# A hybrid decoder layer on one core: the PSUM banks of the recursive products in a ring of five, the others in a ring of three

## The chip, the cores and the metric

The kernel runs on one core of one Trainium2 chip. The metric is the device time of one execution in microseconds (us), given as the median of several runs; smaller is better. One execution was recorded by the hardware profiler, and all times of single instructions come from it. TensorE is called PE below, VectorE DVE, ScalarE ACT, GpSimd POOL and SyncE SP.

## The reference

One layer of a decoder trunk with three parallel branches, in float32, for 1024 prompt rows and 8 sample rows (1032 in all, model width 1024):

```
z = x @ w_in                      # (1032 x 1024) @ (1024 x 7680)
xr, yr, q, k, v, xq, g = split(z)
a_out = rg_lru(conv4(xr)) * gelu(yr)
s_out = window_attention(q, k, v)         # 16 heads, 4 kv heads, window 128, sinks
c_out = memory_attention(xq, mem_kv)      # 4 heads of 256, 256 memory rows
merged = sum(sigmoid(g_n + b_n) * (branch_n @ w_branch[n]))
h = LN(alpha * x + merged @ w_out)
y = LN(alpha * h + (silu(h @ w_gate) * (h @ w_up)) @ w_down)     # hidden width 2816
```

The memory keys and values of the prompt, the updated window buffers and the states are outputs as well.

## The kernel before

Each float32 operand is split into a high and a low part, and a product is three matmuls: high by high, high by low, low by high. ACT makes the high part, DVE the low part by a subtraction (`split`, line 77 for the low part). Most products are plain ones, in `mm3` (lines 117 to 119); the projections of the input, most of gate and up, and most of down are recursive ones, in the manner of Strassen and Winograd, with seven block products in place of eight. The program calls one such piece of work a unit: 256 columns of the weight by all 1032 rows.

A unit is seven steps, i = 0 to 6, in `fast_step`. In each step and for each p of 0 and 1, `fast_product` issues 4 x 3 = 12 matmuls of 258 columns (lines 237 to 239) into one PSUM bank; p is one half of the columns. There are three sums for each p. The first, b, collects steps 0, 2, 4 and 6; d collects steps 1 and 5; c is step 3 alone. Between the steps the running sum is copied out: ACT copies b, d and b after steps 0, 1 and 2 (line 263, tiles p1s, p5s and u2s), DVE adds c to p1s after step 3 (line 265, za) and subtracts for zb after step 4 (line 267), DVE adds d to u2s after step 5 (line 270, the last reading of d), and ACT copies b after step 6 (`finish.late`, zb: lines 1608, 1629 and 1648 for gate, down and the projections). So a unit ends with d read by DVE and b read by ACT.

PSUM has eight banks. The program makes one pool of them for the whole kernel, and the method `bank` (line 71) takes a tile from one of four rings, by tag: `BANKS = {"mm": 3, "s": 2, "t": 2, "o": 1}` (line 34). A ring hands its banks out in turn. The sums b are on ring "mm" with three banks, d on "t" with two, c on "s" with two. The single bank "o" serves the smaller tiles that come between: the gate products of the recurrence, the score transposes of the decode rows (dct, line 921, and drt_c, line 872), vt and others. With three banks and two b's a unit, the second b of a unit has the bank of the first b of the unit before it.

The stages, by the recorded execution: the memory's keys and values (0 to 58 us), the projections with the recurrence and the decode rows between them (to 690 us, 30 units, in the order of the list `UNITS`), the first branch products and the memory attention (to 806), the window attention (to 1016), the last branch product, out projection and the plain part of gate and up (to 1245), the recursive part of gate, up and down (`gate_up_down`, to 1824, 28 units), and the last plain part of down with the layer norm (`last_products`, to 1908). A layer that schedules the program decides the order on each engine from the dependences and its own costs; PE's order of the window stage is set by hand. Loads of weights are issued on SP, in half rows of 512 columns.

In `last_products` the sums are called dl, and their first matmul is at line 117; its weights are made on DVE and ACT by lines 1386 and 1387, and its operands g5l, g6l and g7l by line 77. In the memory attention co is the product of the probabilities (cph and cpl) with the values.

Of the kernel before, what the change touches and what calls it, by code (L numbers as in the profile page):

```python
# [10 lines left out]
F32 = mybir.dt.float32  # L11
# [4 lines left out]
PSUM = bass.MemoryType.PSUM  # L16
DRAM = bass.MemoryType.DRAM

P = 128
# [7 lines left out]
NM = 256  # L27
# [11 lines left out]
QN = T // 4  # L39
# [19 lines left out]
class Builder:  # L59
# [9 lines left out]
        return self.slots[which].tile([P, CW[c]], F32R, tag=tag, name=name, bufs=8)[:, :CH[c][1]]  # L69

    def bank(self, tag, name):
        return self.psum.tile([P, 512], F32, tag=tag, name=name, bufs=BANKS[tag])

    def split(self, hi, lo, src):

# [68 lines left out]
    def setup(self):  # L144
        nc, ctx, tc, io = self.nc, self.ctx, self.tc, self.io
        self.cst = ctx.enter_context(tc.tile_pool(name="cst", bufs=1))
        self.psum = ctx.enter_context(tc.tile_pool(name="psum", bufs=1, space=PSUM))
        self.dram = ctx.enter_context(tc.tile_pool(name="scr", bufs=1, space=DRAM))

        self.ident = self.cst.tile([P, P], F32, name="ident")  # L150
        self.ones = self.cst.tile([P, P], F32R, name="ones")
        self.vec = self.cst.tile([P, V_N], F32, name="vec")
        nc.vector.memset(self.ones.bitcast(F32), 1.0 / D)
# [75 lines left out]
    def fast_product(self, st, i, p, ts, ps, opens):  # L229
# [5 lines left out]
        for k in range(4):  # L235
# [2 lines left out]
            mm(sh[:, w], xl, start=False, stop=False)  # L238
            self.last_mm = mm(sl[:, w], xh, start=False, stop=k == 3).ins  # L239

    def fast_step(self, st, i, ts, finish):

        nc, u, scale = self.nc, st["u"], getattr(finish, "scale", 1.0)
        cols = lambda th, p: slice(HT * th + QN * p, HT * th + QN * (p + 1))
        small = lambda tag, p: self.w1.tile([P, QN], F32, tag=tag, name=f"{tag}{u}_{p}", bufs=2)
        if i == 3:
            st["za"] = self.zt(f"za{u}")
        if i == 4:
            st["zb"] = self.zt(f"zb{u}")
        for p in range(2):  # L250
            if i == 0:
                st["b", p] = self.bank("mm", f"ub{u}_{p}")[:, :QN]
            elif i == 1:
                st["d", p] = self.bank("t", f"ud{u}_{p}")[:, :QN]
            elif i == 3:
                st["c", p] = self.bank("s", f"uc{u}_{p}")[:, :QN]
            b, c, d = st.get(("b", p)), st.get(("c", p)), st.get(("d", p))
            ps = {0: b, 1: d, 2: b, 3: c, 4: b, 5: d, 6: b}[i]
            self.fast_product(st, i, p, ts, ps, i in (0, 1, 3))
            add = partial(nc.vector.scalar_tensor_tensor, scalar=scale, op0=ALU.mult, op1=ALU.add)  # L260
            if i in (0, 1, 2):
                st["s", i, p] = small(("p1s", "p5s", "u2s")[i], p)
                self.last_copy = nc.scalar.mul(st["s", i, p], ps, scale).ins  # L263
            elif i == 3:
                add(st["za"][:, cols(0, p)], c, in1=st["s", 0, p])
            elif i == 4:
                self.last_evac = nc.vector.scalar_tensor_tensor(st["zb"][:, cols(1, p)], b, -scale, st["s", 1, p],
                                                                op0=ALU.mult, op1=ALU.subtract).ins
            elif i == 5:
                add(st["za"][:, cols(1, p)], d, in1=st["s", 2, p])  # L270
            else:
                finish.late(st["zb"][:, cols(0, p)], b)
        if i == 6:
            finish.done(st["za"], st["zb"])

# [114 lines left out]
    def mem_kv(self, moving, xs, load, quarters):  # L390


        nc, io = self.nc, self.io
        h = D // 2
        memx, raws, pairs, sums = [], {}, {}, {}
        order = [(f, p) for f in ((0, 0), (0, 1), (1, 1), (1, 0)) for p in range(2)]

        def put(ps, name, m):
            raw = self.ph.tile([P, 256], F32, tag="kvraw", name=f"{name}r{m}", bufs=4)
            nc.scalar.copy(raw, ps)  # L400
            nc.gpsimd.dma_start(self.scr[name][:, m, :], raw)

        def mem_raw(k):
            raws["mem", k] = self.half_raw(io["memT"][:, 2 * k * NM:(2 * k + 2) * NM], 2 * NM, f"mem{k}")

        def mem_split(k):
            raw = raws.pop(("mem", k))
            for i in range(2):
                memx.append(tuple(self.ph.tile([P, NM], F32R, tag="mem", name=f"mem{e}{2 * k + i}", bufs=16)
                                  for e in "hl"))  # L410
                self.split(*memx[-1], raw[:, i * NM:(i + 1) * NM])

        def fetch(n):
            if n < 16:
                src = io["wmk"][n // 2][:, n % 2 * h:(n % 2 + 1) * h]
            else:
                src = io["wmv"][(n - 16) // 2][:, n % 2 * h:(n % 2 + 1) * h]
            raws[n] = self.half_raw(src, h, f"wm{n}r")

        def cut(n):  # L420
            pairs[n] = self.half_pair(f"wm{n}_")
            self.split(*pairs[n], raws.pop(n))

        def key(n):
            m, e = n // 2, n % 2
            if e == 0:
                sums[m] = self.bank("mm", f"mk{m}")[:, :NM]
            hi, lo = pairs.pop(n)
            cols = [slice(i * P, (i + 1) * P) for i in range(4)]
            self.mm3(sums[m], [((hi[:, w], lo[:, w]), memx[4 * e + i]) for i, w in enumerate(cols)], e == 1, e == 0)  # L430

        def value(n):
            g, j = (n - 16) // 4, n % 4
            if j == 0:
                sums[g] = [self.bank("mm", f"mv{g}_{tt}")[:, :256] for tt in range(2)]
            hi, lo = pairs.pop(n)
            cols = [slice(i * 256, (i + 1) * 256) for i in range(2)]
            for tt in range(2):
                xs_ = [tuple(a[:, tt * P:(tt + 1) * P] for a in memx[2 * j + i]) for i in range(2)]
                self.mm3(sums[g][tt], [(x, (hi[:, w], lo[:, w])) for x, w in zip(xs_, cols)], j == 3, j == 0)  # L440

        warm = self.bank("o", "warm")
        for _ in range(WARM):
            nc.tensor.matmul(warm[:, :P], self.ones, self.ones, start=True, stop=True)
        for f in (partial(mem_raw, 0), partial(fetch, 0), partial(mem_raw, 1), partial(mem_raw, 2), partial(fetch, 1),
                  partial(mem_raw, 3), partial(fetch, 2), partial(fetch, 3)):
            f()
        for f in (partial(mem_split, 0), partial(cut, 0), partial(mem_split, 1), partial(mem_split, 2), partial(cut, 1),
                  partial(mem_split, 3)):
            f()  # L450
        due = -3.5
        for n in range(32):
# [12 lines left out]
            if due > 0:  # L465
                due -= next(moving)
            (key if n < 16 else value)(n)
            if 0 < n <= 16 and n % 2 == 0:
                put(sums.pop(n // 2 - 1), "mk", n // 2 - 1)
            if n > 16 and n % 4 == 0:  # L470
                g = (n - 16) // 4 - 1
                for tt, ps in enumerate(sums.pop(g)):
                    put(ps, "mv", 2 * g + tt)
        for tt, ps in enumerate(sums.pop(3)):
            put(ps, "mv", 6 + tt)
# [1055 lines left out]
    def build(self):  # L1531
        nc, tc, io = self.nc, self.tc, self.io
# [7 lines left out]
        pool = lambda name, side="left": tc.tile_pool(name=name, bufs=1, side=side, reuse_waits="tile")  # L1540
        self.wpool = self.ctx.enter_context(pool("wpool"))
        self.ctx.enter_context(pool("edge", "right")).tile([P, 8], F32, name="edge")
        self.zbufs = 9
        with pool("tp", "right") as self.tp, pool("w1") as self.w1, pool("z") as self.z, ExitStack() as late:
            self.project(late, pool)
        self.act, self.merged, self.first_gates = {}, {}, []
        with ExitStack() as right:
            slots = right.enter_context(ExitStack())
# [36 lines left out]
            with pool("zf") as self.z:  # L1585
                with ExitStack() as tx:
                    self.g, self.wl, self.wraw, self.A = [], [], [], {}
                    with pool("lnp") as self.ph:
# [2 lines left out]
                            h = self.out_proj(self.merged)  # L1591
                        self.tx = tx.enter_context(pool("tx", "right"))
                        ts = self.plain(h)
                    with pool("w1") as self.w1:
                        self.gate_up_down(ts)
                    with pool("ph5") as self.ph:
                        self.last_products()

# [178 lines left out]
```

## Time and profile before

| what | value |
|---|---|
| median of three runs | 1907.44 us (1907.36, 1907.44, 1909.93) |
| the profiled execution, whole | 1909.41 us |
| its span, first to last instruction | 1907.6 us |
| PE's mean granted clock | 0.997 |
| instructions in the span | 38153 |
| moved by DMA | 302.18 MB, 158 GB/s on the mean |

The profiled execution is 1909.41 - 1907.6 = 1.8 us longer than its span: that is time before the first and after the last recorded instruction. Rows of a timeline begin with the start and the length in us, then the engine, the line, the operation, output and inputs by their names, the shape of the output, how many instructions are merged (x2), and in brackets the idle time ahead of the row and what ended it. Rows of the list of waits name an engine and a line, what it waited for, the total in us, how often, and the longest. Rows of a group have the count, the busy time and mean ns, and behind the second bar the idle time ahead of it. Rows of windows have the stretch, its length, the busy time of PE, PE's weight loads, DVE, ACT and POOL, then PE's granted clock, the DMA share, and GB/s.

### The profile page before, as it was taken

Reading aid. Unit: us, or ns where it says so; the run is one execution under the profiler, and the core shown is the slowest. Engines: PE = TensorE matmul, PEld = TensorE weight load, DVE = VectorE, ACT = ScalarE, POOL = GpSimd, SP = SyncE. Lnnn points to the kernel's source line nnn. Section 1 sums busy time; section 2 is a strip of 40 time slices with the busy share of each in tenths; the row PEclk is TensorE's granted clock in tenths of the full one; section 3 lists DMA queues with packets and bytes.
Section 4 is the critical chain, followed back from the end, with each engine's and each line's share of the span. In section 5 each row is a group of like instructions: output and inputs, shape, how many; then the busy total and the mean of one; then the engine's idle time right before and its main releaser. Section 6 shows DMA issues by size and latency. Waiting matters only on the chain.

```text
span 1907.6 us, 38153 instructions
## 1 busy us (share of the span) xinstructions
PE 1889.4 (99%) x14878; PEld 1870.0 (98%) x14878; DVE 1389.9 (73%) x2712; ACT 1014.8 (53%) x2124; POOL 112.8 (6%) x190
## 2 busy tenths in 40 slices
PE   9999999999999999999999999999999999999998
PEld 8999999999999999999999999999999999999997
DVE  7868877977887657578887467786666667858486
ACT  6555564555665656578775234543433433636354
POOL 1000000010000000022210000000000000001200
PEclk9999999999999999999999999999999999999998
DMA  8535434546444368546435351133355335759872
GB/s 316 171 119 173 136 128 139 172 144 214 136 150 147 113 209 264 181 144 208 144 100 164 111 190 51 57 122 118 111 165 191 106 123 177 269 127 272 174 211 90
DMA packets 175973, 302.18 MB, mean 158 GB/s; under 512 B 18912, under 2 KB 92592, under 8 KB 175792
## 3 DMA queue, kind: packets, MB, share of 16 engines
q1 hardware_dynamic: 169120, 280.64, 45.0%
q0 software_dynamic: 4224, 14.78, 3.9%
q10 hardware_dynamic: 2448, 4.33, 0.6%
q8 instruction: 116, 1.90, 0.4%
q14 instruction: 65, 0.53, 0.1%
HBM read 217.97 MB, written 85.89 MB: 159 GB/s over the span
## 4 chain that ended last, share of the span: by engine, by line
PE 90%; DMA 4%; DVE 3%; ACT 2%; issue 1%; SPq 0%; DVEq 0%; ACTq 0%
PE ub L237 5%; PE ub L239 5%; PE ub L238 5%; PE ubfg L238 4%; PE ubfg L237 4%; PE ubfg L239 4%; PE ud L239 3%; PE ud L237 3%; PE ud L238 3%; PE udfg L237 2%; PE udfg L238 2%; PE udfg L239 2%; PE ubf L237 2%; PE op L117 2%; PE ubf L238 2%; PE ubf L239 2%
## 5 line engine op out<-in xcount | busy, mean ns | idle before, releaser
L645 ACT ACTIVATE bp<-bp,bst 128x257 f32<-128x257 f32 (+1 forms) x128 | 62.8, 493 | 38.5 <-DVE bst L639 37.8
L237 PE MATMUL ub<-th,u_0h 128*128 128x258 f32 x240 | 68.6, 286 | 1.0 <-ACT zb L1648 1.0
L237 PE MATMUL ub<-th,u_6h 128*128 128x258 f32 x240 | 68.7, 286 | 0.0
L237 PE MATMUL ub<-th,u_4h 128*128 128x258 f32 x240 | 68.0, 283 | 0.7 <-ACT u2s L263 0.7
L237 PE MATMUL ub<-th,u_2h 128*128 128x258 f32 x240 | 68.0, 283 | 0.4 <-ACT p1s L263 0.4
L239 PE MATMUL ub<-th,u_0l 128*128 128x258 f32 x240 | 68.0, 283 | 0.0
L639 DVE CUSTOM_DVE_ANT_0 bp<-bs,mask,nsnk 128x256 f32<-128x256 f32 (+1 forms) x128 | 55.8, 461 | 16.8 <-PE bs L636 16.4
L239 PE MATMUL ud<-th,u_5l 128*128 128x258 f32 x240 | 68.0, 283 | 0.0
L237 PE MATMUL ud<-th,u_5h 128*128 128x258 f32 x240 | 67.9, 283 | 0.0
L239 PE MATMUL ud<-th,u_1l 128*128 128x258 f32 x240 | 67.9, 283 | 0.0
L239 PE MATMUL ub<-th,u_2l 128*128 128x258 f32 x240 | 67.9, 283 | 0.0
L239 PE MATMUL uc<-th,u_3l 128*128 128x258 f32 x240 | 67.9, 283 | 0.0
L239 PE MATMUL ub<-th,u_6l 128*128 128x258 f32 x240 | 67.9, 283 | 0.0
L239 PE MATMUL ub<-th,u_4l 128*128 128x258 f32 x240 | 67.9, 283 | 0.0
L237 PE MATMUL uc<-th,u_3h 128*128 128x258 f32 x240 | 67.9, 283 | 0.0
L237 PE MATMUL ud<-th,u_1h 128*128 128x258 f32 x240 | 67.9, 283 | 0.0
L238 PE MATMUL ub<-tl,u_0h 128*128 128x258 f32 x240 | 67.6, 282 | 0.0
L238 PE MATMUL ub<-tl,u_6h 128*128 128x258 f32 x240 | 67.5, 281 | 0.0
L238 PE MATMUL ub<-tl,u_2h 128*128 128x258 f32 x240 | 67.4, 281 | 0.0
L238 PE MATMUL uc<-tl,u_3h 128*128 128x258 f32 x240 | 67.4, 281 | 0.0
L238 PE MATMUL ud<-tl,u_5h 128*128 128x258 f32 x240 | 67.4, 281 | 0.0
L238 PE MATMUL ud<-tl,u_1h 128*128 128x258 f32 x240 | 67.4, 281 | 0.0
(949 smaller groups left out, 8294.8 us busy)
## 6 DMA issues: line engine op xcount, KB each, us to landing
ur<-win SPq DMA_DIRECT2D x120, 256.0 KB, 3.2
urfg<-wgu SPq DMA_DIRECT2D x80, 256.0 KB, 2.8
scr_f<-G SPq DMA_DIRECT2D x22, 516.0 KB, 3.1
f<-scr_f SPq DMA_DIRECT2D x16, 516.0 KB, 4.9
fs<-scr_t SPq DMA_DIRECT2D x16, 516.0 KB, 5.5
dck<-cmk SPq DMA_DIRECT2D x32, 256.0 KB, 4.1
dcv<-cmvT SPq DMA_DIRECT2D x32, 256.0 KB, 4.2
urf<-wdn SPq DMA_DIRECT2D x32, 256.0 KB, 2.9
```

Source lines behind the costliest of these rows:

```text
L117: nc.tensor.matmul(ps, sh, mh, start=opens and i == 0, stop=False)
L237: mm(sh[:, w], xh, start=opens and k == 0, stop=False)
L238: mm(sh[:, w], xl, start=False, stop=False)
L239: self.last_mm = mm(sl[:, w], xh, start=False, stop=k == 3).ins
L639: nc.vector.tensor_tensor_reduce(pg[g], s[:, u * 256:u * 256 + n], msk, 1.0, snk[:, g:g + 1], ALU.add, ALU.min, st[:, g:g + 1])
L645: nc.scalar.activation(x, x, AF.Exp, bias=st[:, g:g + 1], scale=-1.0, accum_out=st[:, 4 + g:5 + g])
```

## The change

In the two stages with units, eight banks are divided otherwise. Five banks, x0 to x4, hold b and d of the units and, ahead of the first unit, the sums of the memory's keys and values. They lie in a queue `self.idle`: `take` removes the one at its front, which was handed back longest ago, and a unit hands its d banks back with step 5 and its b banks with step 6, at the back. All other tiles, c of the units, the recurrence, the transposes, are on one ring of three banks, "s".

Since the tags of the tiles differ between the stages, the one pool becomes four: psum0 for the projections, psum1 for the attentions and branch products, psum2 for gate, up and down, psum3 for the last stage. A pool's banks are opened again in the next one, and a tile waits there for the last reader of the old tile in the same bank. In psum1 and psum3 the four old tags with their counts are used.

```diff
     def bank(self, tag, name):
+        if self.idle is not None:
+            return self.psum.tile([P, 512], F32, tag="s", name=name, bufs=3)
         return self.psum.tile([P, 512], F32, tag=tag, name=name, bufs=BANKS[tag])
+
+    def take(self, name):
+        k = self.idle.popleft()
+        return k, self.psum.tile([P, 512], F32, tag=f"x{k}", name=name, bufs=1)
...
-        self.psum = ctx.enter_context(tc.tile_pool(name="psum", bufs=1, space=PSUM))
...
+    def sum_bank(self, st, tag, name):
+
+        if self.idle is None:
+            return self.bank(tag, name)[:, :QN]
+        k, ps = self.take(name)
+        st.setdefault("banks", []).append(k)
+        return ps[:, :QN]
...
             if i == 0:
-                st["b", p] = self.bank("mm", f"ub{u}_{p}")[:, :QN]
+                st["b", p] = self.sum_bank(st, "mm", f"ub{u}_{p}")
             elif i == 1:
-                st["d", p] = self.bank("t", f"ud{u}_{p}")[:, :QN]
+                st["d", p] = self.sum_bank(st, "t", f"ud{u}_{p}")
...
+        if self.idle is not None and i > 4:
+            self.idle += st["banks"][2:] if i == 5 else st["banks"][:2]
...
-            nc.scalar.copy(raw, ps)
+            nc.scalar.copy(raw, bank[1][:, :256])
+            self.idle.append(bank[0])
...
+        banks = lambda name: tc.tile_pool(name=name, bufs=1, space=PSUM, reuse_waits="tile")
         with pool("tp", "right") as self.tp, pool("w1") as self.w1, pool("z") as self.z, ExitStack() as late:
-            self.project(late, pool)
+            with banks("psum0") as self.psum:
+                self.idle = deque(range(5))
+                self.project(late, pool)
+        self.idle, psum = None, ExitStack()
+        self.psum = psum.enter_context(banks("psum1"))
...
-                    with pool("w1") as self.w1:
+                    psum.close()
+                    with pool("w1") as self.w1, banks("psum2") as self.psum:
+                        self.idle = deque(range(5))
                         self.gate_up_down(ts)
+                    self.idle, self.psum = None, self.ctx.enter_context(banks("psum3"))
```

On PE, at the border of the fourth and the fifth unit of the projections: ub4_1 is b of p=1, ud4_0 and ud4_1 are d. Before, the first matmul into each bank waits for the engine that emptied it:

```order
L239 MATMUL ub4_0_2099<-th0_0_122,u4_0l_1975 128x258
L237 MATMUL ub4_1_2114<-th0_1_124,u4_0h_1974 128x258 [waits Activation_49]
...
L239 MATMUL ub4_1_2114<-th0_1_124,u4_0l_1975 128x258
L237 MATMUL ud4_0_2145<-th1_0_126,u4_1h_2010 128x258 [waits DVE_49]
...
L237 MATMUL ud4_1_2160<-th1_1_128,u4_1h_2010 128x258 [waits DVE_49]
```

With the change, at the same place:

```order
L244 MATMUL ub4_0_2099<-th0_0_122,u4_0l_1975 128x258
L242 MATMUL ub4_1_2114<-th0_1_124,u4_0h_1974 128x258 [waits DVE_49]
...
L244 MATMUL ub4_1_2114<-th0_1_124,u4_0l_1975 128x258
L242 MATMUL ud4_0_2145<-th1_0_126,u4_1h_2010 128x258 [waits DVE_49,Activation_49]
...
L242 MATMUL ud4_1_2160<-th1_1_128,u4_1h_2010 128x258 [waits Activation_49]
```

The order of the matmuls is the same. The second b now follows DVE, which read d of the unit before, and the first d follows two engines. Over the program 49 more waits of this kind, each a semaphore instruction of its own, stand in PE's order, 46 of them at d.

On PE, at the first sum of the last stage, behind the last unit (ubf13_1). Before:

```order
L239 MATMUL ubf13_1_23574<-dth16_1_22774,uf13_6l_23694 128x258
L117 MATMUL dl0_0_23898<-g5h21_23479,wl0h00_23677 128x258 [waits Activation_49]
L118 MATMUL dl0_0_23898<-g5l21_23480,wl0h00_23677 128x258
...
L117 MATMUL dl0_0_23898<-g6h0_23589,wl0h00_23677 128x258 [waits Activation_49]
L118 MATMUL dl0_0_23898<-g6l0_23590,wl0h00_23677 128x258 [waits DVE_49]
```

With the change:

```order
L244 MATMUL ubf13_1_23582<-dth16_1_22782,uf13_6l_23702 128x258
L123 MATMUL dl0_0_23910<-g5h21_23487,wl0h00_23685 128x258 [waits DVE_49,Activation_49]
L124 MATMUL dl0_0_23910<-g5l21_23488,wl0h00_23685 128x258
...
L123 MATMUL dl0_0_23910<-g6h0_23597,wl0h00_23685 128x258 [waits Activation_49]
L124 MATMUL dl0_0_23910<-g6l0_23598,wl0h00_23685 128x258
```

The first matmul of dl0_0 now waits for DVE too; the later wait for DVE ahead of g6l0 is gone, since what the first one waits for stands behind g6l0 in DVE's order.

On DVE, at the start of the memory attention: M is the merged sum, mkl, mv and cql the low parts of keys, values and queries, wba2 the weights of a branch. Before:

```order
L721 SCALAR_TENSOR_TENSOR M1_9557<-gta1_9660,bra1_1_9766 128x390 [waits PE_49]
L77 TENSOR_TENSOR mkl0_9872<-mkl0_9872,mkh0_9871 128x512 [waits DMAHW4_49,Activation_49]
L77 TENSOR_TENSOR mv0_9874<-mv0_9874 128x512 [waits DMAHW5_49,Activation_49]
L721 SCALAR_TENSOR_TENSOR M0_9556<-gta0_9620,bra0_2_9832 128x258 [waits PE_49]
L77 TENSOR_TENSOR cql0_9877<-cql0_9877,cqh0_9876 128x1024 [waits DMAHW6_49,Activation_49]
L77 TENSOR_TENSOR wba20_l_9996<-wba2r0__9993,wba20_h_9995 128x512 [waits DMAHW0_49,DVE_49,Activation_49]
```

With the change:

```order
L83 TENSOR_TENSOR mkl0_9876<-mkl0_9876,mkh0_9875 128x512 [waits DMAHW4_49,Activation_49]
L83 TENSOR_TENSOR mv0_9878<-mv0_9878 128x512 [waits DMAHW5_49,Activation_49]
L737 SCALAR_TENSOR_TENSOR M1_9561<-gta1_9664,bra1_1_9770 128x390 [waits PE_49]
L83 TENSOR_TENSOR cql0_9881<-cql0_9881,cqh0_9880 128x1024 [waits DMAHW6_49,Activation_49]
L83 TENSOR_TENSOR mkl1_9949<-mkl1_9949,mkh1_9948 128x512 [waits DMAHW7_49,Activation_49]
L83 TENSOR_TENSOR wba20_l_10000<-wba2r0__9997,wba20_h_9999 128x512 [waits DVE_49,DMAHW0_49,PE_49,Activation_49]
```

The two additions to M move behind splits of the memory operands, and the split of the second head's keys comes ahead of that of the branch weights.

More of the change, by code (lines that the diff above doesn't have):

```diff
@@ L396, in mem_kv, with put @@
         order = [(f, p) for f in ((0, 0), (0, 1), (1, 1), (1, 0)) for p in range(2)]
-        def put(ps, name, m):
+        def put(bank, name, m):
             raw = self.ph.tile([P, 256], F32, tag="kvraw", name=f"{name}r{m}", bufs=4)
-            nc.scalar.copy(raw, ps)
+            nc.scalar.copy(raw, bank[1][:, :256])
+            self.idle.append(bank[0])
             nc.gpsimd.dma_start(self.scr[name][:, m, :], raw)
@@ L426, in key @@
             if e == 0:
-                sums[m] = self.bank("mm", f"mk{m}")[:, :NM]
+                sums[m] = self.take(f"mk{m}")
             hi, lo = pairs.pop(n)
             cols = [slice(i * P, (i + 1) * P) for i in range(4)]
-            self.mm3(sums[m], [((hi[:, w], lo[:, w]), memx[4 * e + i]) for i, w in enumerate(cols)], e == 1, e == 0)
+            self.mm3(sums[m][1][:, :NM], [((hi[:, w], lo[:, w]), memx[4 * e + i]) for i, w in enumerate(cols)], e == 1, e == 0)
         def value(n):
@@ L434, in value @@
             if j == 0:
-                sums[g] = [self.bank("mm", f"mv{g}_{tt}")[:, :256] for tt in range(2)]
+                sums[g] = [self.take(f"mv{g}_{tt}") for tt in range(2)]
             hi, lo = pairs.pop(n)
@@ L439, in value @@
                 xs_ = [tuple(a[:, tt * P:(tt + 1) * P] for a in memx[2 * j + i]) for i in range(2)]
-                self.mm3(sums[g][tt], [(x, (hi[:, w], lo[:, w])) for x, w in zip(xs_, cols)], j == 3, j == 0)
+                self.mm3(sums[g][tt][1][:, :256], [(x, (hi[:, w], lo[:, w])) for x, w in zip(xs_, cols)], j == 3, j == 0)
         warm = self.bank("o", "warm")
```

## The prediction

> **What bounds the kernel now.** First the busy shares on the page and the engines in the chain that ended last, then the windows cut at the stage borders, then what PE waits for.
>
> ```profile
> PE 1889.4 (99%) x14878; PEld 1870.0 (98%) x14878; DVE 1389.9 (73%) x2712; ACT 1014.8 (53%) x2124; POOL 112.8 (6%) x190
> ```
> ```profile
> PE 90%; DMA 4%; DVE 3%; ACT 2%; issue 1%; SPq 0%; DVEq 0%; ACTq 0%
> ```
> ```profile
> 60.00:690.00 630.00, 627.58 (x5175) 625.30 (x5174) 487.70 (x998) 361.00 (x685) 36.18 (x49) 1.00 0.46 149
> 690.00:806.00 116.00, 114.77 (x747) 107.92 (x746) 75.52 (x169) 69.93 (x172) 3.64 (x9) 1.00 0.70 232
> 1245.00:1824.00 579.00, 578.91 (x4810) 578.64 (x4809) 391.99 (x597) 254.88 (x494) 19.08 (x22) 1.00 0.55 166
> 1824.00:1908.00 84.00, 74.38 (x615) 73.74 (x614) 60.75 (x120) 39.13 (x88) 1.80 (x2) 0.94 0.40 123
> ```
> ```profile
> PE ub L237 <- ACT zb L1648: 1.0, 1, 1.0
> PE co L118 <- DVE cpl L77: 0.7, 2, 0.4
> PE dct L921 <- ACT ti L829: 0.2, 1, 0.2
> ```
>
> TensorE is the bound: 99% busy, 90% of the chain, at a granted clock of 1.00 in the stages that the change touches (the first number after POOL's in a windows row). Those are the projections (60 to 690 us, 30 units) and gate/up/down (1245 to 1824 us, 28 units). In them PE is idle for 630.00 - 627.58 = 2.4 us and 579.00 - 578.91 = 0.1 us. So freeing banks earlier can only return small holes; the longest bank wait of the whole list is the first of the three rows, 1.0 us.
>
> Busy time hides a part of each hole, because matmul rows overlap: a 258-column matmul lasts 0.28 us, yet the next starts 0.12 us later. So I read holes from start to start, less 0.12.
>
> **Part 1: b's second bank is no longer b's first bank of the unit before.** In the kernel before, the bank of p=0 of step 0 is taken again 24 matmuls after its last write, 24 x 0.12 = 2.9 us; in that time ScalarE must have copied it out. With five banks every reuse of the units stands at least 48 matmuls away, 5.8 us. Where does the old distance fall short? In the timeline of PE, the matmul ahead, the one that waits, and at the first place the one behind:
>
> ```profile
> 100.25 0.28 PE L239 MATMUL ub<-th,u_0l 128*128 128x258 f32 x1
> 101.56 0.39 PE L237 MATMUL ub<-th,u_0h 128*128 128x258 f32 x1 [1.04 <-ACT zb L1648]
> 101.79 0.29 PE L238 MATMUL ub<-tl,u_0h 128*128 128x258 f32 x1
> ...
> 228.70 0.28 PE L239 MATMUL ub<-th,u_0l 128*128 128x258 f32 x1
> 228.88 0.39 PE L237 MATMUL ub<-th,u_0h 128*128 128x258 f32 x1
> ...
> 268.31 0.28 PE L239 MATMUL ub<-th,u_6l 128*128 128x258 f32 x1
> 268.76 0.38 PE L921 MATMUL dct<-ident,dcs 128*8 128x128 f32 x2 [0.17 <-ACT ti L829]
> ...
> 274.15 0.28 PE L238 MATMUL ud<-tl,u_1h 128*128 128x258 f32 x1
> 274.32 0.39 PE L237 MATMUL ub<-th,u_0h 128*128 128x258 f32 x1
> ...
> 335.25 0.28 PE L237 MATMUL ub<-th,u_0h 128*128 128x258 f32 x1
> 335.60 0.38 PE L872 MATMUL drt_c<-ident,qdc 128*8 128x128 f32 x2
> ...
> 376.96 0.28 PE L239 MATMUL ub<-th,u_0l 128*128 128x258 f32 x1
> 377.21 0.39 PE L237 MATMUL ub<-th,u_0h 128*128 128x258 f32 x1
> ...
> 1562.21 0.29 PE L239 MATMUL ubfg<-hh,ufg_0l 128*128 128x258 f32 x1
> 1562.34 0.28 PE L237 MATMUL ubfg<-hh,ufg_0h 128*128 128x258 f32 x1
> 1562.46 0.28 PE L238 MATMUL ubfg<-hl,ufg_0h 128*128 128x258 f32 x1
> ...
> 1582.44 0.28 PE L239 MATMUL ubfg<-hh,ufg_0l 128*128 128x258 f32 x1
> 1582.82 0.39 PE L237 MATMUL ubfg<-hh,ufg_0h 128*128 128x258 f32 x1
> ```
> ```profile
> 101.15 0.36 ACT L1648 ACTIVATE zb<-ub 128x258 f32<-128x258 f32 x1
> ```
>
> At 101.56 the hole is 101.56 - 100.25 - 0.12 = 1.19 us, and the row behind comes 0.23 after it instead of 0.12, 0.11 more for refilling: 1.30 us. ScalarE's copy of that bank ends at 101.15 + 0.36 = 101.51, 0.05 ahead, so this is the bank. The other step-0 matmuls are read alike, each with the same 0.11 (an estimate from 101.79): 228.88 gives 0.06 + 0.11 = 0.17, 274.32 gives 0.05 + 0.11 = 0.16, 377.21 gives 0.13 + 0.11 = 0.24, 1582.82 gives 0.26 + 0.11 = 0.37. The transposes dct (0.45 - 0.12 = 0.33) and drt_c (0.35 - 0.12 = 0.23) wait for the single bank "o", whose place a ring of three takes. Together 1.30 + 0.17 + 0.16 + 0.24 + 0.37 + 0.33 + 0.23 = 2.8 us. Most of the boundaries between units have no hole: that at 1562.34 stands 0.13 behind the row ahead, and its next 0.12. What comes late next, once these waits are gone, is the split of the weight quarters; at none of these places is it the wait named. I take -2.8, with the ends 0 (a split is late too) and -9.5 (a rival below).
>
> **Part 2: a bank that the last stage takes too early.** The old kernel's first output sum of the last stage, dl, opened on a ring of three that was long free. Now the last pool is opened anew, its first bank is the physical bank of the last unit's d for p=0, and dl waits for DVE's read of that (the L270 row):
>
> ```profile
> 1823.82 0.28 PE L239 MATMUL ubf<-dth,uf_6l 128*128 128x258 f32 x1
> 1823.93 0.28 PE L117 MATMUL dl<-g5h,wl0h 128*128 128x258 f32 x1
> ```
> ```profile
> 1800.22 0.42 DVE L270 SCALAR_TENSOR_TENSOR zaf<-udf,u2sf 128x258 f32<-128x258 f32 x1
> ...
> 1820.98 2.37 DVE L77 TENSOR_TENSOR g7l<-g7l,g7h 128x1032 fp32r<-128x1032 f32 x2
> 1823.27 1.66 DVE L1387 SCALAR_TENSOR_TENSOR wl0l<-wl1r,wbar,wl0h 128x128 fp32r<-128x128 f32 x6
> 1824.84 0.75 DVE L270 SCALAR_TENSOR_TENSOR zaf<-udf,u2sf 128x258 f32<-128x258 f32 x2
> ```
>
> That read stands in DVE's queue behind splits of 2.37 and 1.66 us. The first of the pair starts at 1824.84 and takes 0.42 by the single row of it, to 1825.26; with the same 0.05 for release dl starts at 1825.31 instead of 1823.93, 1.38 later, and refills for 0.11: +1.5 us. Queued behind dl on PE is the whole last stage, and nothing else is there to fill the hole. If PE comes 2.8 us earlier and DVE's splits do not, since they follow DMAs, the hole grows by that, to 4.3; if DVE's queue drains before PE arrives, it is 0. The last three rows follow each other without a gap, so DVE is behind by work and not by a wait; the holes that go lie 240 us and more ahead of this place, time enough for loads and splits to move up with PE. So I take 1.5, with the ends 0 and 4.3. Each microsecond is paid once: PE is in the chain there.
>
> **Part 3: waits on two engines.** The ring mixes banks that DVE frees with banks that ScalarE frees, so 46 first matmuls of d now wait for both. Instructions with two such waits are already in the kernel: of the 60 of this row 32 wait for two engines.
>
> ```profile
> L673 PE MATMUL bo<-bph,vs 128*128 128x512 f32 x60 | 24.0, 400 | 0.2 <-ACT bph L76 0.2
> ```
>
> All 60 have 0.2 us of idle time ahead of them, 0.2 / 60 = 3 ns each; 46 x 3 ns = 0.15 us at most, taken as 0. The Trainium skill, "Perfetto Trace Analysis", section "Identifying Dependency Chains", says that an instruction that waits on several engines may get extra EventSemaphore instructions ahead of it, which speaks against the change. The trace has the row above against a price for it; what it would be with a price is a rival.
>
> **Part 4: order.** The scheduler draws some DVE, ScalarE and SP rows otherwise: around the ninth to the eleventh unit and at the start of memory attention (706 to 760 us). On PE only transposes and a few rows of one or two units move. DVE is busy 75.52 of 116.00 us there, so a moved row usually fits; the cpl row above shows two waits of 0.7 us together. I take 0, with 1.4 to either side: twice what co now waits for cpl.
>
> **Sum.** -2.8 + 1.5 + 0 + 0 = -1.3 us. The profiled execution took 1909.41, 1907.6 of it span and 1.8 outside; so 1908.1 on its scale. The median of the three runs is 1907.44, 1.97 below the profiled execution, so 1906.1 in a measurement like that one; I say 1906.0.
>
> **The rivals.** A change of 0.2% (3.8 us) is about what a measurement of this kernel can tell from none: faster begins under 1903.6, slower over 1911.3.
>
> Likeliest, a near cancel, as summed: 1906.0, chance 0.52.
>
> Holes return as split waits: the weight quarter that comes after is then the late one, gain 0, and dl costs 1.5: 1907.44 + 1.5 = 1908.9. For it: a wait for p1s and u2s on ScalarE exists in other rows; against: nothing at the places in Part 1 is late but the bank. Chance 0.16.
>
> The dl wait does not come, since DVE is ahead or the bank is another: 1907.44 - 2.8 = 1904.6. For it: DVE would only have to reach that row 1.4 us earlier, less than one of the splits of 2.37 and 1.66 ahead of it. Against: in the trace the read begins 0.9 us after dl's place (1824.84 against 1823.93), and the change moves nothing out of that queue. Chance 0.11.
>
> Small bubble at each unit border: if each of 56 borders cost 0.17 (228.88, the smallest such hole), the ring would bring 56 x 0.17 = 9.5 instead of 2.8: 1907.44 - 9.5 + 1.5 = 1899.4. Against it stand rows such as 1562.34, at 0.13. For it, that the 0.12 itself may hold a part. The Trainium skill, "Perfetto Trace Analysis", section "Optimization Strategy", says that the same gap repeating can mean too little PSUM for the next tile; by the row at 1562.34 the trace has no such repeated gap. Chance 0.12.
>
> The double waits cost: the extra instruction cannot be done ahead of time, and the pipeline of PE gets a bubble at each of the 46, 0.17 as at 228.88: 7.8 us. 1906.0 + 7.8 = 1913.8. It decides from 0.17 x 46 > 5.3, that is from 0.12 us a wait. Against it is the L673 row at 3 ns. Chance 0.05. That is the mechanism on the other side.
>
> The order at memory attention makes co late: DVE's splits (cpl) run after the reordered ones, and each of the eight half heads waits as long as the longest of the two waits that exist.
>
> ```profile
> 789.94 0.44 PE L117 MATMUL co<-cph,mv 128*128 128x512 f32 x1
> 790.83 0.49 PE L118 MATMUL co<-cpl,mv 128*128 128x512 f32 x1 [0.44 <-DVE cpl L77]
> 791.16 0.40 PE L119 MATMUL co<-cph,mv 128*128 128x512 f32 x1
> 791.40 0.40 PE L117 MATMUL co<-cph,mv 128*128 128x512 f32 x1
> ```
>
> There 790.83 - 789.94 = 0.89 against 0.24 at 791.40, so 0.65, and 0.1 for refilling: 0.75 x 8 = 6.0, 1906.0 + 6.0 = 1912.0. Chance 0.04.
>
> **How the numbers follow.** Faster by over 0.2% is the repeated bubble alone: 0.12. Slower is the two last: 0.09. Within 0.2% are the first three: 0.79. The range goes from 1903.0, the third case with 1.4 of order and a little over, to 1910.5: the second case with 1.4 of order (1910.3), and a dl hole of up to 4.3 with a full gain (1907.44 - 2.8 + 4.3 = 1908.9, and 1.4 of order, 1910.3 again). It leaves out the bubble case and the two slow ones.
>
> **What would show it.** Right: no row of PE waiting on zb (L1648 before) in the list of waits; the hole at about 101.5 is gone, and a new wait of dl for zaf near 1821 to 1824 of about 1.3 us; DVE's list of work there the same. Wrong: PE's start-to-start of 0.12 at the borders getting shorter; new holes at first d matmuls; holes ahead of co in each half head; the last stage with no wait, or one of 3 us or more.

## The result, and the profile after

| | median, us | ratio to the kernel before, 95% interval |
|---|---|---|
| kernel before (8 runs) | 1907.85 (1907.08 to 1909.93) | |
| changed kernel (8 runs) | 1912.95 (1912.34 to 1915.47) | 1.0026 [1.0017, 1.0035] |
| the same, profiled execution | 1913.14, span 1911.0 | |

The change makes the kernel slower by 5.0 us [3.2, 6.7]. The prediction said 1906.0, between 1903.0 and 1910.5, with 0.79 on no difference; the measured time lies above that range. Ratios, here and below, leave out one execution of the run after_code, at 2261.9 us, that stands far outside the rest.

Busy time and the chain of the changed kernel, first and fourth part of the page:

```profile
PE 1888.3 (99%) x14878; PEld 1869.2 (98%) x14878; DVE 1390.4 (73%) x2712; ACT 1014.3 (53%) x2124; POOL 111.1 (6%) x190
```
```profile
PE 89%; DVE 4%; DMA 4%; ACT 2%; issue 1%; SPq 0%; DVEq 0%; ACTq 0%
```

The engines work as much as before, on the same number of matmuls. The difference must be idle time of PE, and the windows say in which stage. Changed kernel, then the one stretch of the kernel before that the prediction does not show:

```profile
60.00:690.00 630.00, 627.60 (x5187) 626.16 (x5186) 488.28 (x999) 361.89 (x687) 34.49 (x50) 1.00 0.45 149
690.00:806.00 116.00, 112.72 (x731) 105.61 (x730) 74.65 (x164) 68.80 (x171) 3.50 (x9) 1.00 0.70 230
806.00:1016.00 210.00, 208.28 (x1413) 201.21 (x1412) 171.62 (x496) 156.76 (x450) 43.27 (x88) 1.00 0.46 138
1245.00:1824.00 579.00, 578.71 (x4807) 578.35 (x4807) 391.73 (x597) 253.56 (x488) 19.08 (x22) 1.00 0.54 166
1824.00:1911.00 87.00, 76.39 (x635) 75.61 (x634) 63.06 (x124) 41.17 (x94) 1.80 (x2) 0.96 0.42 128
```
```profile
806.00:1016.00 210.00, 209.14 (x1418) 202.45 (x1418) 171.42 (x497) 157.65 (x451) 43.08 (x88) 1.00 0.47 140
```

Length less PE's busy time is PE's idle time. In the projections it was 2.42 and is 2.40 us: of the forecast gain of 2.4 nothing is seen in it. Idle time hides a part of each hole; from start to start, the holes over 0.05 us of this stage sum to 6.3 us in the trace before and to 5.1 in this one, half of the forecast gain. In the stage to 806 us PE's idle time went from 1.23 to 3.28, in the windows from 0.86 to 1.72, in gate/up/down from 0.09 to 0.29, and in the last stage from 9.62 to 10.61. So most of the loss lies in two stages whose banks the change leaves on their old rings. The list of waits of the changed kernel names the places:

```profile
PE co L124 <- DVE cpl L83: 1.7, 3, 0.8
PE bo L690 <- DVE bpl L83: 1.6, 3, 0.6
...
PE dl L123 <- ACT wl2h L1402: 1.3, 1, 1.3
PE ub L242 <- DVE zb L280: 1.2, 2, 0.7
PE cs L123 <- ACT cp L527: 1.2, 1, 1.2
...
PE udfg L244 <- DVE ufg_1l L83: 0.3, 1, 0.3
```

The place that carried the forecast gain, in the timeline of PE, the border at 100 us: changed kernel, then a second profiled execution of the kernel before (the run before_again below).

```profile
100.23 0.28 PE L244 MATMUL ub<-th,u_0l 128*128 128x258 f32 x1
100.35 0.29 PE L242 MATMUL ub<-th,u_0h 128*128 128x258 f32 x1
```
```profile
101.04 0.39 PE L237 MATMUL ub<-th,u_0h 128*128 128x258 f32 x1 [0.51 <-ACT zb L1648]
```

The bank wait is gone, as forecast: 0.12 from start to start. But in the second trace the kernel before waits there 0.51 instead of 1.04 us. And at dl, PE and then DVE of the changed kernel:

```profile
1826.25 0.28 PE L244 MATMUL ubf<-dth,uf_6l 128*128 128x258 f32 x1
1827.84 0.36 PE L123 MATMUL dl<-g5h,wl0h 128*128 128x258 f32 x1 [1.31 <-ACT wl2h L1402]
```
```profile
1825.70 1.66 DVE L1403 SCALAR_TENSOR_TENSOR wl0l<-wl1r,wbar,wl0h 128x128 fp32r<-128x128 f32 x6
1827.27 0.75 DVE L283 SCALAR_TENSOR_TENSOR zaf<-udf,u2sf 128x258 f32<-128x258 f32 x2
```

1827.84 - 1826.25 - 0.12 = 1.47 us, with the read of d (L283) behind the splits of wl0l. The list names ACT's wl2h; but 1827.27 plus the 0.42 of one such read is 1827.69, 0.15 ahead of dl, and the runs with another bank settle it below.

### The profile page after: what moved, and what is told of

It is laid out like the page before. It is cut to its first block, busy times and chain, and to the rows that moved or that the text cites. A ratio compares the mean times of both kernels' runs of the same rounds, so it can differ in the third digit from the quotient of the medians.

```text
span 1911.0 us, 38196 instructions
## 1 busy us (share of the span) xinstructions
PE 1888.3 (99%) x14878; PEld 1869.2 (98%) x14878; DVE 1390.4 (73%) x2712; ACT 1014.3 (53%) x2124; POOL 111.1 (6%) x190
## 4 chain that ended last, share of the span: by engine, by line
PE 89%; DVE 4%; DMA 4%; ACT 2%; issue 1%; SPq 0%; DVEq 0%; ACTq 0%
PE ub L244 5%; PE ub L242 5%; PE ub L243 5%; PE ubfg L243 4%; PE ubfg L244 4%; PE ubfg L242 4%; PE ud L244 3%; PE ud L242 3%; PE ud L243 3%; PE udfg L244 2%; PE udfg L242 2%; PE udfg L243 2%; PE op L123 2%; PE op L125 2%; PE op L124 2%; PE brs L123 2%
## 5 line engine op out<-in xcount | busy, mean ns | idle before, releaser
L243 PE MATMUL ub<-tl,u_4h 128*128 128x258 f32 x240 | 67.4, 281 | 0.0
```

## The experiments

All times are medians; a ratio is to the kernel before in the same set of runs, estimated from all executions, so it need not be the quotient of two medians. The kernel before stood at 1908.68 us in the set of split, order_new, order_old and dl_bank, at 1908.67 in that of before_again, after_again, ring_early and ring_late, at 1907.86 in that of sp_shift (five executions, all others eleven), order_bank and order_bank_shift, and at 1908.48 in that of after_code, order_bank_code and before_code. A "hole" is the time from one matmul's start to the next, less what is usual for its shape (0.12 us for 258 columns); sums of holes take those over 0.05 us. Each run gives one trace.

| run | median, us | ratio, 95% interval |
|---|---|---|
| before_again | 1908.70 | 0.9996 [0.9987, 1.0005] |
| after_again | 1912.66 | 1.0022 [1.0013, 1.0031] |
| split | 1909.88 | 1.0007 [0.9999, 1.0016] |
| order_new | 1909.51 | 1.0006 [0.9997, 1.0015] |
| order_old | 1912.02 | 1.0012 [1.0003, 1.0021] |
| dl_bank | 1910.79 | 1.0009 [1.0000, 1.0018] |
| ring_early | 1911.91 | 1.0017 [1.0008, 1.0026] |
| ring_late | 1912.44 | 1.0019 [1.0010, 1.0028] |
| order_bank | 1909.73 | 1.0009 [1.0000, 1.0018] |
| sp_shift | 1913.83 | 1.0032 [1.0020, 1.0045] |
| order_bank_shift | 1911.35 | 1.0019 [1.0010, 1.0028] |
| after_code | 1911.57 | 1.0017 [1.0008, 1.0026] |
| order_bank_code | 1909.33 | 1.0003 [0.9994, 1.0012] |
| before_code | 1910.77 | 1.0016 [1.0007, 1.0025] |

None beats the kernel before. The second trace of the kernel before has 0.66 at the border near 101 us where the first had 1.19. The second trace of the changed kernel repeats the holes at dl (1.48 for 1.47), udfg and bo; that near 224 us (0.67) is gone and the one ahead of cs falls from 1.35 to 0.22.

**Is the order of memory attention the cost, and who changes it?** Theory: the loss between 690 and 806 us is DVE's and ACT's new order. Rival: the loss comes with the ring. The run split cuts the one pool of the kernel before into two, with the old rings in both:

```diff
-        self.psum = ctx.enter_context(tc.tile_pool(name="psum", bufs=1, space=PSUM))
...
-            self.project(late, pool)
+            with banks("psum0") as self.psum:
+                self.project(late, pool)
+        self.psum = self.ctx.enter_context(banks("psum1"))
```

> The kernel before with one edit: the pool of PSUM banks is closed after the projections and opened anew, with the old rings; no ring of five. On VectorE the rows at the start of the memory attention then stand as in the changed kernel; PE's order is as before. Order theory (the loss of the changed kernel between 690 and 880 us, 3.6 us, is paid by that order, with cs and co waiting): 1907.85 + 2.7 to 3.7 = 1910.6 to 1911.6. Early theory (PE came 2 us earlier out of the projections and met loads that did not): no ring, so no loss, 1907.9. Bank theory (the reopened pool's banks are freed too late): as the order theory, 1910.6 to 1911.6.

order_new is the kernel before with the changed kernel's order of DVE and ACT at that place, order_old the changed kernel with the old order; both pin it with a table of positions in the program:

```diff
+        for engine, rows in QUEUE.items():
+            traced = [i for i in nc.cur_bb.bb.instructions if i.engine == engine]
+            for m, n in zip(rows, rows[1:]):
+                self.behind(traced[n], traced[m])
```

> The kernel before, with one pool and its old rings, in which 60 rows of VectorE and 44 of ScalarE at the start of the memory attention are put into the order that they have in the changed kernel. Order theory: 1907.85 + 2.7 to 3.7 = 1910.6 to 1911.6. Early theory and bank theory: no change, 1907.9.

> The changed kernel, in which the same rows of VectorE and ScalarE are put back into the order of the kernel before; ring and pools stay. Order theory: 1912.95 - 2.7 to 3.7 = 1909.3 to 1910.3, with the holes ahead of cs and co gone. Early theory and bank theory: no change, 1912.9.

In split DVE has the new order at memory attention, though no bank of the units is on a new ring: the border between the pools makes the order. What it costs is seen on DVE and PE just ahead of the second head's scores. First PE and DVE of the changed kernel, then DVE of the kernel before, of split and of order_old:

```profile
719.19 0.39 PE L123 MATMUL cs<-mkh,cqh 128*128 128x256 f32 x1 [1.19 <-ACT cp L527]
```
```profile
716.25 1.22 DVE L83 TENSOR_TENSOR cql<-cql,cqh 128x1024 fp32r<-128x1024 f32 x1 [0.79 <-ACT cqh L82]
717.40 0.68 DVE L524 TENSOR_REDUCE cst<-cs 128x2 f32<-128x512 f32 x1
```
```profile
717.20 0.69 DVE L508 TENSOR_REDUCE cst<-cs 128x2 f32<-128x512 f32 x1
717.80 1.22 DVE L77 TENSOR_TENSOR cql<-cql,cqh 128x1024 fp32r<-128x1024 f32 x1
```
```profile
714.99 1.23 DVE L77 TENSOR_TENSOR cql<-cql,cqh 128x1024 fp32r<-128x1024 f32 x1 [0.78 <-ACT cqh L76]
716.13 0.68 DVE L507 TENSOR_REDUCE cst<-cs 128x2 f32<-128x512 f32 x1
```
```profile
715.11 0.68 DVE L527 TENSOR_REDUCE cst<-cs 128x2 f32<-128x512 f32 x1
715.71 1.21 DVE L86 TENSOR_TENSOR cql<-cql,cqh 128x1024 fp32r<-128x1024 f32 x1
```

In the new order the reduction of the first head's scores (cst) stands behind the split of the next queries (cql). That split waits 0.79 us for ACT and then takes 1.22, the exponential on ACT (cp) waits for cst, and the next scores cs wait for cp. In the old order cst goes first. The hole ahead of that cs:

| kernel | hole ahead of cs, us |
|---|---|
| before, before_again, before_code | 0.00, 0.00, 0.00 |
| order_old, order_bank, order_bank_shift | 0.00, 0.00, 0.01 |
| order_bank_code | 0.00 |
| split, order_new, ring_late | 0.88, 0.92, 0.91 |
| ring_early, dl_bank, sp_shift | 0.67, 1.19, 0.83 |
| after, after_again, after_code | 1.35, 0.22, 0.00 |

So the old order has no such hole in seven traces; the new one has it in eight of nine. In after_code DVE stands in the same new order, but PE comes to cs 2.93 us after the split of cql began, where without its hole the changed kernel would come after 1.59, and meets no hole. The co behind it loses up to 0.75 in the same way (cpl behind cql), and 1.11 in after_code, where cql waits 1.71 us for ACT. The holes of the whole stage sum to 4.35 us on the mean of the seven kernels with the old order (3.80 to 5.33) and to 5.82 of the nine with the new one (4.80 to 6.72): +1.5 us. The times agree as far as they reach: split +1.3 us [-0.2, 3.1], order_new +1.1 [-0.6, 2.9], less than the 2.7 to 3.7 expected and each not told from nothing, and order_old +2.3 [0.6, 4.0] where the changed kernel shows +4.2 to +5.0. The rival falls for these holes, as split has them without the ring.

**The bank of dl.** One tile is taken from the reopened pool and left unused, so that dl has another bank, idle since the unit before the last:

```diff
+                    self.bank("t", "first")
```

> The changed kernel, in which the last pool hands out two banks before the first sum of the last stage, so that this sum gets a bank that has been idle for a unit. All theories: the hole of 1.47 us ahead of dl goes, 1912.95 - 1.5 = 1911.4, unless the last stage is bound elsewhere and gives the gain back, 1912.9.

PE at the same place:

```profile
1827.99 0.28 PE L244 MATMUL ubf<-dth,uf_6l 128*128 128x258 f32 x1
1828.11 0.28 PE L123 MATMUL dl<-g5h,wl0h 128*128 128x258 f32 x1
```

The hole is 0, and DVE's read of d (L283) now starts at 1829.02, 0.91 us after dl has begun. ACT's wl2h, which the list had named, runs here from 1827.37 to 1829.22, past the start of dl as well. The cause was the bank, and the name in the list the wrong one of two. The time falls to +1.7 us [0.0, 3.4], by more than 1.5, but the intervals hold 1.5.

**The ring in one stage alone.** ring_early has the ring in the projections alone, ring_late in gate/up/down alone:

```diff
-                        self.idle = deque(range(5))
+                        self.idle = None
```

> The changed kernel with the ring of five in the projections alone; the later pools use the old rings. Its order is that of the changed kernel up to 1245 us; the last stage's first sum falls on a bank that ScalarE frees 1.3 us late. Project theory (what the ring moves in the projections, the zb waits and the bo wait, is most of the loss): as the changed kernel, +4.5 us, 1913.2. Later theory (the ring in gate, up and down costs): as with the pool split alone, +1.2 us, and +1.3 for dl, 1911.2.

> The changed kernel with the ring of five in gate, up and down alone; the projections use the old rings in a pool of their own. Project theory: the pool split's 1.2 us and the dl wait of 1.5, with 0.1 net from the ring: +2.8 us, 1911.5, and no wait for zb near 223 and 415 over 0.3 us. Later theory: +4 to 5 us, 1913.

Each alone costs about what both cost, so the two costs do not add up stage by stage. Both keep the four pools, and with them the order at memory attention; both keep a wait at dl, 2.02 us in ring_early, whose first bank was read last by ACT, and 1.47 in ring_late.

**Order and bank together.** order_bank is order_old with the unused tile of dl_bank.

> The changed kernel with both single repairs, the old order of VectorE and ScalarE at the memory attention and an idle bank for the first sum of the last stage. Sum theory (each part costs what its holes show): the changed kernel's +4.5 us less 1.9 and 1.5: +1.1 us over before, 1909.8. If the parts hide each other: +2.5 us or more.

Without both, +1.7 us [0.0, 3.4] is left, at the edge of what can be told from nothing; the traces show one more place.

**The window attention.** In the kernels with the ring in the projections the holes between 806 and 1016 us sum to 7.61 us on the mean (8 kernels, the two with fewer PE instructions below not counted), in the six without it to 6.56: +1.05. Most of it is one hole ahead of one and the same matmul of bo, the 36th, near 867 us: 0.72 to 1.04 us in seven of the eight and 0.41 in order_bank_shift, and 0.40 at most in the other six. PE and ACT of after_again, then the six issues on SP that load bcL (shortest, median and longest in ns), and of the DMA queues between 857.9 and 858.95 the one that fetches code:

```profile
867.34 0.50 PE L690 MATMUL bo<-bpl,vs 128*128 128x512 f32 x1 [0.77 <-DVE bpl L83]
```
```profile
860.83 0.52 ACT L82 CAST bcH<-bcL 128x384 fp32r<-128x384 f32 x1 [2.70 <-DMA bcL<-scr_c]
```
```profile
L134 SPq DMA_DIRECT2D bcL<-scr_c x6: 320/390/1249, 856.3 to 860.1; - x6
```
```profile
q8 instruction: 1, 0.02, 5.6%
```

The same ACT row and issues of the kernel before, and its DMA queues between 857.4 and 860.7, where q1 has the only line:

```profile
860.10 0.51 ACT L76 CAST bcH<-bcL 128x384 fp32r<-128x384 f32 x1 [0.92 <-DMA bcL<-scr_c]
```
```profile
L128 SPq DMA_DIRECT2D bcL<-scr_c x6: 320/372/543, 857.4 to 860.2; - x6
```
```profile
q1 hardware_dynamic: 696, 0.73, 77.9%
```

One issue takes 1.25 us where the median is 0.39 and the longest before was 0.54. The load lands later, ACT waits 2.70 in place of 0.92, its work on the bcH and bph tiles is late, and bo waits for bpl. What is different beside that issue is one packet of 16 KB on the queue "instruction", q8: a piece of the program itself, being fetched. In all sixteen traces, SP issues longer than 0.85 us number 22 to 27 a trace, and 14 to 19 of them overlap such a packet; of some 945 shorter ones 42 to 66 do. The hole does not follow the length of the issue: with one of 1.19 us order_bank_shift has 0.41 at that bo, with one of 1.26 the first trace of the changed kernel has 0.72, and before_again has 0.40 with none above 0.7.

Two ways to move it were tried. sp_shift and order_bank_shift put 12 small loads on SP at the start of the program, so that each later load is another one in SP's program:

```diff
+        for n in range(12):
+            pad = self.cst.tile([1, 8], F32, name=f"pad{n}")
+            nc.sync.dma_start(pad, io["vec"][0:1, 8 * n:8 * n + 8])
```

> The changed kernel with 12 loads of 32 bytes into spare tiles on SyncE's queue, early in the projections; PE, VectorE and ScalarE keep their order, and all later instructions of SyncE stand 12 places or more further on. Place theory (in the five kernels with the ring in the projections one DMA issue of SyncE, a load for branch c, takes 1.25 to 1.98 us instead of 0.36, always near its 845th instruction, and another on a load for the decode rows near its 400th; where such a long issue falls goes by the place in SyncE's program): the long issues fall on other instructions, the holes ahead of bo near 867 (1.0) and of step 6 near 415 (0.6 to 1.2) fall below 0.4 us, 1 to 2 us faster than the changed kernel, +2.5 to +3.5 us over before. Load theory (PE meets loads that are late for another reason): both holes as in the changed kernel, +4.5 us.

> Both repairs, and the 12 small loads on SyncE. Place theory: the holes near 415 and 867 go too, so 1 to 2 us below the run with both repairs alone: 0 to -1 us against before, 1908. Load theory: as the run with both repairs, +1.1 us.

In sp_shift the long issue stays with the same load (the 845th of SP before, the 857th now), and the bo hole with it, 1.04: its place in SP's program is not the cause. Both times are spoiled by another effect, told at the end.

The other way changes the number of PE's instructions. The program opens with 20 matmuls that only warm PE, whose result nothing reads; after_code and order_bank_code make them 4 wider ones, before_code 36 narrower ones in the kernel before:

```diff
-WARM = 20
+WARM = 4
...
-            nc.tensor.matmul(warm[:, :P], self.ones, self.ones, start=True, stop=True)
+            nc.tensor.matmul(warm, self.ones, self.ones[:, None, :].to_broadcast([P, 4, P]), start=True, stop=True)
```

> The changed kernel with 4 warm-up matmuls of 512 columns in place of 20 of 128; nothing else moves. Code theory (a 16 KB code packet of PE that falls on a load's issue holds SyncE's queue): with 16 matmuls and their weight loads less, the packets come 1 to 2 us later against the work, at 859.5 to 861 and 406.5 to 407.5; the holes ahead of bo near 867 (1.0) and of step 6 near 415 (0.6 to 1.2) fall below 0.4 us, 1 to 1.8 us faster than the changed kernel: +3.0 us over before. Rival (something else of the ring): both holes as before, +4.5 us.

> Both repairs (old order at the memory attention, idle bank for the first sum of the last stage) and the 4 long warm-up matmuls. Code theory: 1 to 1.8 us below both repairs alone (+1.8 us): +0.4 us or less against before. Rival: +1.8 us, both holes there.

> The kernel before with 36 warm-up matmuls of 64 columns in place of 20 of 128. Code theory: the packets come 1 to 2 us earlier against the work, at about 859 and 407.5, and the hole ahead of bo near 867, 0.0 and 0.4 in its two traces, grows to 0.7 to 1.0: 0.5 to 1 us slower than before. Rival: no new hole, same time.

The same six issues of after_code, then of before_code:

```profile
L134 SPq DMA_DIRECT2D bcL<-scr_c x6: 320/376/543, 860.1 to 863.0; - x6
```
```profile
L128 SPq DMA_DIRECT2D bcL<-scr_c x6: 319/384/1286, 858.2 to 861.9; - x6
```

With 16 fewer matmuls ahead, the packet comes after these issues (863 to 864 us), none is long, and that bo has no hole, in both such kernels. With 16 more in the kernel before, the packet falls on them (859.32) and one takes 1.29 us, as in the changed kernel, though the hole that follows is smaller, 0.28. The other traces agree: in nine of the sixteen the packet starts ahead of the last of these six issues, and one of the six takes 1.19 to 2.01 us; in the other seven it starts during the last of them or later, and none takes over 0.55. So where the fetch of PE's program falls decides whether those issues are long. The holes of this stage fall to 6.67 and 6.32 in after_code and order_bank_code, as in kernels without the ring. The time that this gains is not resolved: by the ratios after_code is lower by 1.0 us than after_again, and order_bank_code by 1.1 than order_bank, both within their intervals. With order, bank and code all moved, order_bank_code stands at +0.6 us [-1.1, 2.3], which is not told from the kernel before. Other holes came: order_bank_code has one of 1.87 near 415 us, after_code two of 1.1 to 1.2 ahead of co, and its projections begin at 58.46 us where the two traces of the changed kernel have 57.45 and 57.21. before_code, slower by 3.1 us [1.3, 4.8], is not explained: its bo hole accounts for 0.28 of it.

The same pattern may stand behind the waits of ub for zb near 415 us (0.58 to 1.87 in nine of the ten kernels with the ring in the projections, 0.29 at most in the six with the old one). DVE and SP of the changed kernel:

```profile
413.20 0.42 DVE L917 SCALAR_TENSOR_TENSOR dcj<-dcv,dcvq 128x256 f32<-128x256 f32 x1 [1.42 <-DMA dcv<-cmvT]
...
414.70 0.42 DVE L280 SCALAR_TENSOR_TENSOR zb<-ub,p5s 128x258 f32<-128x258 f32 x1
```
```profile
407.00 0.89 SPq L902 DMA_DIRECT2D dcvq<-dcpd  x1
```

A decode row on DVE waits for its load, zb stands behind it in the queue, and PE waits for zb. One SP issue took 0.89 us in place of some 0.35, with a q8 packet in that stretch. Against it stand two traces: order_bank_code has the longest of these waits, 1.87 us, with no SP issue above 0.51 between 405 and 412 us, and after_code has an issue of 1.51 at 410.63 and no hole. So the cause of these waits stays open.

## Why the prediction was wrong

Three steps failed. Part 1 put the gain at 2.8 us, of which 2.4 in the projections; the holes there fell by 0.7. Part 4 put the new order at 0; it costs 1.5 us of holes. And the sum had no term for the window attention, where the holes grew by 1.05, because Part 3 looked for the price of the added waits only at the matmuls that wait.

**Part 1, -2.8: the mechanism right, the size not.** The waits for the banks went; the fixed ones (dct 0.33, drt_c 0.23) are in the traces of the old rings and not in those of the ring. But the largest term, 1.30 at 101.56, was one execution's. In six traces with the old ring in the projections that hole was 1.19, 0.66, 0.10, 0.75, 0.67 and 0.30. Why it differs so from trace to trace was not followed. The warning was on the table: the profiled execution was 1.97 us over the median, and the prediction subtracted its holes and then also moved it onto the median, which counts the same time twice as far as these holes made that execution long. And the ring brought waits of its own near 415 us. Over the stage, holes sum to 5.74 us on the mean of those six and to 5.02 of the ten kernels with the ring: -0.7, where -2.4 was forecast.

**Part 2, +1.5: right.** 1.47, by the row and the queue named; 0 with another bank.

**Part 3, 0: right where it looked.** The 46 first matmuls of d show no hole at PE. The rule of the Trainium skill ("Perfetto Trace Analysis", "Identifying Dependency Chains"), that such waits can bring EventSemaphore instructions, was given no price, and PE's rows agree. What they do change is the length of PE's program, and so when its code is fetched. The Trainium skill, "Runtime: NRT & Kernel Launch", section "Instruction fetch mechanics", says that code is refilled in blocks of 16 KiB, 256 instructions, and calls the cost "mostly hidden". The trace agrees on the size: 16 KB packets, and from one to the next PE begins 254 to 258 instructions (matmuls, weight loads and waits) on the median of each trace. On the cost the measurement differs: an issue of SP beside such a packet took 1.25 us in place of 0.39, and a hole of 1.03 followed at PE. The traces also tell what moved the packets. That near 860 us starts, in all sixteen, when PE has begun 13469 to 13503 instructions, while the matmul of bo with the hole, the 36th, is the 13567th instruction in the kernel before and the 13588th in the changed one. The 21 more are waits, 19 of them in the projections, so the same packet falls 21 instructions earlier in the work. With the 16 fewer warm-up matmuls of after_code that bo is the 13556th.

**Part 4, 0 with 1.4 to either side: wrong, +1.5.** It rested on DVE being busy 75.52 of 116.00 us, an average that says nothing of a row with a late operand put ahead of one that PE waits for. The rival of co named the stage and foresaw 6.0 by a hole at each of eight half heads; there are one or two new ones in most traces, and the first is at cs.

**The sum.** -0.7 of the ring in the projections, +1.5 of the order, +1.05 in the windows, some +0.2 in gate/up/down (an 0.45 hole ahead of udfg in each kernel that reopens the pool there, less the bank waits that went) and +1.5 of dl give +3.5 us, by holes; measured are +5.0 [3.2, 6.7] and, in the second set, +4.2 [2.5, 5.9]. About 1 us is not placed. In the traces themselves nothing is missing: the span, less the start of the projections and the holes behind it, is 1828.5 to 1829.4 us in all fourteen kernels without the 12 small loads. From the first trace before to the first after the span grew by 3.4 us and the holes by 3.8, in the second pair by 2.0 and 1.9. What is not placed lies between traces and medians: the two profiled executions of the kernel before are 1.6 and 0.6 us over their medians, those of the changed kernel 0.2 over and 1.4 under. The terms also fit most runs that keep only some of them: 1.5 for split and order_new (measured +1.3 and +1.1), 3.2 for ring_late (+3.6), 4.0 for ring_early (+3.2), 2.0 for order_old and dl_bank (+2.3 and +1.7), 0.5 for order_bank (+1.7), all inside the intervals; for before_code (+3.1) they have nothing. That is no independent test, since the terms are means over these same traces.

## What to carry to other kernels

Before a single hole is priced, look at it in a second trace of the same code, or leave it out of the gain by as much as the profiled execution lies over the median. A border between pools is a change of its own: it can reorder engines that it does not touch, and its first tile should not take the bank that was read last. In this kernel, bound to 99% by one engine, holes of about 1 us (0.05%) come and go with where code fetches meet loads; a gain of that size is to be looked for with the count of instructions varied too.

## What the runs showed that was not expected

With 16 more narrow matmuls, whose result nothing reads, before_code stands at 1.0016 [1.0007, 1.0025], though its projections start as before, at 57.20 against 57.16 us. Most of that is not explained.

In sp_shift and order_bank_shift, with 12 tiny tiles and loads more, 258-column matmuls follow each other after 120.30 ns on the mean of the unbroken ones, and after 120.06 to 120.08 in all others. Over the some 12,000 of them that is 0.23 x 12,000 = 2.8 us, more than these two runs were to tell apart. Whether the moved addresses or the loads do it was not tried.
